# A fused MLP kernel by Strassen products: when the next x is cast, and where two weight sums stand

## The chip, the cores and the metric

The kernel runs on one core of a Trainium2 chip. The metric is device time in microseconds (us) from the first to the last instruction of one execution. The kernel before takes 1495.97 us, the median of three runs (1494.37 to 1496.18).

A core has TensorE (PE, matrix products into PSUM banks), VectorE (DVE), ScalarE (ACT) and GpSimd (POOL) as its computing engines, and SyncE (SP), which here only issues DMA transfers. Each engine works through its own instructions in order and waits on semaphores for the others. POOL issues transfers too: those that convert the type on the way (float32 to float16), and the stores of results.

## The reference

```python
h = x @ w1
h = 0.5 * h * (1 + np.tanh(np.sqrt(2 / np.pi) * (h + 0.044715 * h ** 3)))
return (h @ w2).astype(np.float32)
```

x is 8 x 1024 x 1024, w1 1024 x 4096 and w2 4096 x 1024, all float32. So it is two large matrix products with a gelu between them, over 8192 rows.

## The kernel before

The 8192 rows are taken in eight super-blocks (`sb`) of 1024. For each, `matmul1` makes g = gelu(x @ w1), kept in SBUF as float16, and then a second stage makes g @ w2. The second stage is `matmul2_made` for the first two super-blocks and `matmul2` for the others.

Every product is done in Strassen's manner: a matrix is cut into 2 x 2 blocks, called "11", "12", "21" and "22", and seven products of block sums replace eight of blocks. The products are numbered 1 to 7. The sums of weight blocks are in `W_SUM`: sum 5 is 12 - 11, sum 6 is 22 - sum 5, sum 7 is 22 - 12, sum 4 is 21 - sum 6. Those on the other side are in `S_SUM` and in `XOps.make`. Sums of weights are written w, those of x are written x, and those of g are written g below. Nearly all of these sums, and the adds that put the products together, go through the helper `tt` on line 119 to DVE. Copies from PSUM go through `act_copy` on line 135 to ACT. Loads and stores on SP go through `load_in_order` on line 132.

The order of the work on each engine is written out by hand: `tc.keep_in_program_order` pins an instruction to its place, and a table (`FILL`, and `FILL_2` for the later stages) says which extra job follows which product. A key such as `51` means: after product 5, group 1. In the first super-block and in the second, each product of the second stage has four groups (`NQ` = 4) of 16 matmuls, one group for each 128 rows.

**The start.** `First` loads the first x, transposes it on PE and loads the first weight columns. `First.pair` does the first pair of column chunks with plain products. While it runs, its function `sums` makes the x sums and the sums of the second pair of weight columns ("pair two", `(2, 2)`), in a fixed order on DVE. Then `matmul1` goes on with its loop over pairs `j` (16 chunks, 8 pairs). In one turn PE makes products 1 and 2 for both chunks of the pair, then 5, 6, 3 and 7; product 4 follows in the next turn (`late`). DVE adds products 1 and 2 together (`add(a[h], banks_b[h])`, the "chain sums"), ACT applies gelu to that and copies the other products out of PSUM. `jobs` are weight sums for later turns; the first `half` of them are put behind the chain sums and the rest at the end of the turn. For j = 1 of the first super-block `half` is 0 before.

**The second stage of the first super-block.** `matmul2_made` takes w2 in blocks: `bring` loads a block's float32 data into staging buffers (transfers `u<-in_w_dram`, 512 KB each, eight for a block) and casts each to float16. Blocks 11 and 21 are cast by POOL, block 12 by ACT, and block 22, which is brought after product 1, by ACT too. `keep` stores a cast block to `raw2_d` in DRAM (transfers `raw_d<-u`, four of 512 KB for a block), from where later stages load it. All of these are issued by SP in the order in which they are written. The seven products come in the order 1, 2, 5, 6, 3, 7, 4. Product 6 needs sum 6, so it needs block 22: jobs w60 to w63 make the four pieces of that sum after products (5, 0) and (5, 1). `post` copies a group's result out of PSUM on ACT (products 1, 5, 6 and 4) or adds it on DVE (2, 3, 7), and stores finished rows from POOL.

In the same stage the next x is made ready: `x_cast` (line 405) issues, from POOL, eight transfers that read the next 1024 rows as float32 and write them as float16 to a DRAM buffer `xb`. `after` names an instruction behind which they are placed. `x_transpose` then issues, from SP, sixteen transposing transfers from `xb` into the four x blocks. Jobs x5, x7, x6, x3 make the x sums of the next super-block; q5, q6, q7 and q4 make its first weight sums, out of a `MadeQuad` whose raw blocks are loaded from DRAM when product 3 is done (order 12, 11, 22, 21); i2 and i3 make sums of sums.

Of the kernel before, what the change touches and what calls it, by code (L numbers as in the profile page):

```python
# [29 lines left out]
def slots(table):  # L30
# [5 lines left out]
    ;20:g50 w50 w51;21:g51 w52;22:w53 g52;23:g53 p14  # L36
    ;50:w60 w61;51:w62 w63;52:g30 g31;53:g32 g33
    ;60:w70 w71;61:w72 w73;62:w40 w41;63:w42 w43
    ;70:x5;73:x7;40:x6 x3;41:q5 q6;42:q7 q4
    ;43:i2 i3""".replace("\n    ", "")),  # L40
    slots("""10:g60 w50;11:g61 w51;12:g62 w52;13:g63 w53
    ;20:g50 p55;21:g51 p56;22:g52 p57;23:g53 p54
# [19 lines left out]
def kernel(  # L62
# [7 lines left out]
    nc = tc.nc  # L70
# [38 lines left out]
    def psum():  # L109
        return pp.tile([P, HT], F32, name="ps")  # L110

    def temp():
        return tp.tile([P, HT], F32, name="tmp")

    def unit(rows, cols):
        return up.tile([P, rows, cols], DT, name="u")
# [9 lines left out]
    def flat(t):  # L126
        return t.rearrange("p a b -> p (a b)")
# [3 lines left out]
    def load_in_order(out, in_, **kw):  # L131
        return tc.keep_in_program_order(nc.sync.dma_start(out=out, in_=in_, **kw))  # L132

    def act_copy(out, in_):
        tc.keep_in_program_order(nc.scalar.copy(out=out, in_=in_))  # L135
# [8 lines left out]
    def columns(t, c, n=1):  # L144

        h, c = divmod(c, 2)
        return t[:, h * KH:(h + 1) * KH, c * P:(c + n) * P]
# [148 lines left out]
    def x_blocks():  # L296
        return {b: unit(KH, HT) for b in ("22", "21", "12", "11")}
# [8 lines left out]
    class First:  # L306
# [53 lines left out]
        def pair(self, gelu):  # L360


            def plain(bank, a, b, c, part=None):
                cols = slice(None) if part is None else slice(part * HT // 2, (part + 1) * HT // 2)
                for r in (1, 2):
                    w = columns(self.quad.raw[f"{r}{b}"], c)
                    for k in range(KH):
                        tc.keep_in_program_order(nc.tensor.matmul(  # L368
                            bank[:, cols], lhsT=w[:, k, :], rhs=self.xs.blocks[f"{a}{r}"][:, k, cols],
                            start=r == 1 and k == 0 and not part,  # L370
                            stop=r == 2 and k == KH - 1,
                            skip_group_check=bool(part),
                        ))

            def sums(h):
                for m in ("x5", "w5", "x7", "x6", "w6", "x3", "w7", "w4"):
                    if m[0] == "x":
                        self.xs.make(int(m[1]), cols=slice(h * HT // 2, (h + 1) * HT // 2), pin=True)
                    elif h == 1:
                        self.quad.sum(int(m[1]), (2, 2), True)  # L380

            for q in range(3):
                self.cast(1, q)
            for b, c in ((1, 0), (1, 1), (2, 0), (2, 1)):
                bank = psum()
                plain(bank, 1, b, c)
                if b == 2:
                    self.transpose(1, c)
                gelu(f"1{b}", c, bank)
            self.cast(1, 3)  # L390
            self.transpose(1, 2)
            banks = {(c, b): psum() for c in range(2) for b in (1, 2)}
            for part in range(2):
                for c in range(2):
                    for b in (1, 2):
                        plain(banks[c, b], 2, b, c, part)
                        if part:
                            gelu(f"2{b}", c, banks[c, b])
                    if c == 0 and not part:
                        self.transpose(1, 3)  # L400
                    if part != c:
                        self.more[part]()
                sums(part)

    def x_cast(s, after, rows=range(0, SB, P), xb=None):
        if xb is None:
            xb = xdram.tile([SB, H], DT, name="xb")
        with tc.issue_after(after.ins):
            for q in rows:
                nc.gpsimd.dma_start(out=xb[q:q + P, :], in_=x2[s * SB + q:s * SB + q + P, :])  # L410
        return xb
# [6 lines left out]
    def x_transpose(xb, dma, blocks=None, which=range(4)):  # L418
        blocks = blocks or x_blocks()
        for b, t in [list(blocks.items())[i] for i in which]:  # L420
            a, k = int(b[0]) - 1, int(b[1]) - 1
            for j in range(KH):
                dma(
                    t[:, j, :],
                    xb[a * HT:(a + 1) * HT, (k * KH + j) * P:(k * KH + j + 1) * P],
                    transpose=True,
                )
        return blocks
# [3 lines left out]
    def matmul1(xs, sb, quads, start=None):  # L432
# [69 lines left out]
        def ahead(j):  # L502

            if sb > 1 or j // 2 == NI // QC - 1:
                return ()
            q, second = divmod(j, 2)
            if not second:
                quad = MadeQuad(q + 1, sb == 0, sb == 1)
                quads.append(quad)
                if sb == 0:  # L510
                    quad.load()
                    quads[q].keep_raw()
            quad = quads[q + 1]
            if sb == 0:
                return [lambda m=m: quad.sum(m, pin=True) for m in SUMS] if second else ()
            jobs = [lambda m=m: quad.sum(m, pin=True) for m in ((7, 4) if second else (5, 6))]
            if sb == 1:
                if second:
                    jobs += [lambda m=m: quad.inner_sums(m) for m in INNER_1]
            return jobs  # L520
# [21 lines left out]
        for j in range(NI // 2):  # L542
# [11 lines left out]
            jobs = list(ahead(j))  # L554
# [5 lines left out]
            banks_c, p5, t = [], [], [temp(), temp()]  # L560
# [27 lines left out]
            difference(j - 1)  # L588
            half = (len(jobs) + 1) // 2
            if start is not None and j == 1:  # L590
                half, jobs, rest = 0, jobs[:2], jobs[2:]
            elif start is not None and j == 2:
                half, jobs = 2, rest
            if sb == 1:
                half = 3 if j % 2 else 0
# [94 lines left out]
    def matmul2_made(sb, g, keep_w1, xb):  # L690
# [24 lines left out]
        def keep(b):  # L715
            if sb == 0:
                for q in range(NI // QC):
                    load_in_order(raw2_d[q][:, BLOCKS.index(b), :], flat(raw[b][q]))
# [13 lines left out]
        def pieces(m):  # L732
            return raw[W_TERM[m]] if m in W_TERM else sums[m]

        def rows(t, q):
            return t[:, :, q * P:(q + 1) * P]

        s2, a, p5, t6, at = {}, {}, {}, {}, {}
# [47 lines left out]
        for m, name, first in (  # L786
            (1, "a", True), (2, "b", True), (5, "c", True), (6, "a", False),
            (3, "c", False), (7, "a", False), (4, "a", False),
        ):
            for q in range(NQ):  # L790
                if first:
                    banks[name].append(psum())
                bank = banks[name][q]
                matmuls2(bank, s2[q] if m == 6 else rows(g[operands[m]], q), pieces(m), first)
                post(m, q, bank)
                if (m, q) == (2, 1) and sb == 0:
                    xb = x_cast(sb + 1, at[1])
                if (m, q) == ((5, 0) if sb else (6, NQ - 1)):
                    xs = XOps(x_transpose(xb, load_in_order))
                if (m, q) == (3, NQ - 1) and sb == 0:  # L800
                    quad = MadeQuad(0, False, True)
                if (m, q) == (4, 0) and sb:
                    quad = StoredHalf(0)
                if (m, q) == (1, NQ - 1) and sb == 0:
                    sums[5] = [unit(2, HALF) for _ in range(NI // QC)]
                    for t in sums[5]:
                        act_copy(t[:, 0, :1], warm)
                    bring("22", act_copy, True)
                    for b in ("21", "12", "22"):
                        keep(b)  # L810
                run((m, q))
        return xs, [quad]

# [125 lines left out]
    def matmuls2(bank, a, pieces, first):  # L939
        for c in range(NI):  # L940
            tc.keep_in_program_order(nc.tensor.matmul(  # L941
                pair(bank),
                lhsT=a[:, c, :],
                rhs=chunks(pieces[c // QC])[:, :, c % QC, :],
                start=(first and c == 0),
                stop=(c == NI - 1),
                skip_group_check=not first,
            ))
# [75 lines left out]
    pace = consts.tile([P, 2], DT, name="pace")  # L1024
# [3 lines left out]
    xs, quads = first.xs, [first.quad]  # L1028
    for sb in range(NSB):
        g, early, nxt = matmul1(xs, sb, quads, first if sb == 0 else None)  # L1030
        if sb < 2:
            xs, quads = matmul2_made(sb, g, None if sb else quads[-1].keep_raw, nxt)
            continue
        matmul2(sb, g, early, nxt)
        if nxt is not None:
            xs, quads = nxt, [StoredHalf(0)]
# [30 lines left out]
```

## Time and profile before

| what | value |
|---|---|
| median of three runs | 1495.97 us |
| profiled execution, span | 1493.1 us |
| PE busy | 1478.2 us (99%) |
| DVE busy | 1148.6 us (77%) |
| ACT busy | 613.3 us (41%) |
| POOL busy | 226.9 us (15%) |
| HBM traffic | 313 GB/s over the span |

Where the stages lie in the span: the first multiplication of the first super-block ends and the second begins at 113.5 us; that one ends at 216.0 us; the second super-block follows, with its second multiplication from 312.9 to 409.6 us.

How to read it. Matmuls are pipelined, and their ends are modelled, so a busy PE is not a PE at its peak; but a gap in PE is time lost, as PE is busy nearly all the time. An engine's idle time costs nothing unless PE waits for it in the end. In the waits, a row names who waited, then who ended the wait, the total in us, how often, and the longest. In the timeline, "x4" means four instructions merged into one row, and the brackets give the idle time of the engine before it and what ended that. In the chain that ended last, each row is a start, a duration, and what the time was spent on. q1 is the queue of the transfers that SP issues, q0 that of those that POOL issues. The granted clock is the share of TensorE's full clock.

### The profile page before, as it was taken

The page shows a single profiled execution, that of the slowest core. Times are in us where ns is not written, and L with a number is a line of the kernel's source. Part 1 is how long each engine was busy: PE and PEld are TensorE (multiplying, and loading weights), DVE is VectorE, ACT ScalarE, POOL GpSimd, SP SyncE. Part 2 cuts the span into 40 slices and gives each one's busy share as a digit, 9 for nine tenths or more (in the row PEclk, how much of TensorE's full clock was granted, in tenths as well). Part 3 has the DMA queues.
Part 4 walks back from the last instruction along what each step waited for, and adds up shares of the span by engine and source line. Part 5 has one row for each costly group of instructions (what it writes and reads, how often), then busy time and mean ns, then how long its engine had stood idle before and what let it go on. Part 6 is the DMA issues. An engine that isn't in the chain of part 4 may idle for free.

```text
span 1493.1 us, 26323 instructions
## 1 busy us (share of the span) xinstructions
PE 1478.2 (99%) x9879; PEld 962.9 (64%) x9879; DVE 1148.6 (77%) x1792; ACT 613.3 (41%) x1154; POOL 226.9 (15%) x310
## 2 busy tenths in 40 slices
PE   8999899999999999999999999999999999999998
PEld 4444344444455788557875588755886568855687
DVE  5656448757667899778987799877997779877787
ACT  5664216531066411664126621366214652156510
POOL 2542022312311011110122001210011101101011
PEclk9999999999999999999999999999999999999999
DMA  9999996996997999999999899999999999997896
GB/s 327 335 342 365 293 333 224 390 299 233 361 309 179 340 294 308 330 219 372 310 316 322 219 381 320 294 320 247 347 303 318 290 257 361 293 375 235 295 280 216
DMA packets 242719, 453.70 MB, mean 304 GB/s; under 512 B 80672, under 2 KB 85792, under 8 KB 241696
## 3 DMA queue, kind: packets, MB, share of 16 engines
q1 hardware_dynamic: 215680, 358.69, 71.5%
q0 software_dynamic: 26912, 93.34, 21.2%
q8 instruction: 77, 1.26, 0.3%
q14 instruction: 50, 0.41, 0.1%
HBM read 355.47 MB, written 111.15 MB: 313 GB/s over the span
## 4 chain that ended last, share of the span: by engine, by line
PE 93%; DMA 4%; DVE 2%; issue 0%; ACT 0%; SPq 0%; DVEq 0%; ACTq 0%
PE ps L438 48%; PE ps L900 34%; PE ps L941 10%; DMA u<-in_w_dram 3%; DVE tmp L119 1%; PE ps L368 1%; DVE u L119 1%; DMA gc<-in_w_dram 1%; DMA u<-w_d 1%; DMA out_dram<-tmp 0%; SPq L132 0%; ACT u L135 0%; PE ps L345 0%; ACT g L451 0%; ACT tmp L135 0%
## 5 line engine op out<-in xcount | busy, mean ns | idle before, releaser
L438 PE MATMUL ps<-u 128*128 128x512 f16 (+1 forms) x4104 | 746.8, 344 | 3.4 <-DVE tmp L119 1.7
L119 DVE TENSOR_TENSOR tmp<-tmp,ps 128x256 f32<-128x256 f32 (+1 forms) x930 | 450.4, 530 | 275.7 <-PE ps L438 174.9
L438 PEld LDWEIGHTS <-u 128*128 128x128 f16 x4104 | 400.9, 98 | 346.7 <-issue 12.4
L135 ACT COPY tmp<-ps 128x512 f32<-128x512 f32 x410 | 231.1, 581 | 295.4 <-PE ps L438 154.1
L451 ACT ACTIVATE g<-tmp 128x512 f16<-128x512 f32 x378 | 238.3, 633 | 166.3 <-DVE tmp L119 166.2
L900 PE MATMUL ps<-u,gc 128*128 128x256 f16 x2688 | 300.4, 273 | 0.0
L900 PEld LDWEIGHTS <-gc 128*128 128x128 f16 x2688 | 262.5, 98 | 31.1
L119 DVE TENSOR_TENSOR u<-u 128x2048 f16<-128x2048 f16 (+3 forms) x292 | 219.6, 791 | 14.8 <-ACT u L135 12.3
L900 PE MATMUL ps<-u,g 128*128 128x256 f16 x2016 | 227.9, 273 | 0.0
L135 ACT COPY u<-ps 128x512 f32<-128x512 f32 (+1 forms) x134 | 77.9, 586 | 347.9 <-PE ps L900 341.0
L900 PEld LDWEIGHTS <-g 128*128 128x128 f16 x2016 | 197.2, 98 | 24.1
L119 DVE TENSOR_TENSOR u<-u,ps 128x512 f32<-128x512 f32 x216 | 147.3, 682 | 35.1 <-PE ps L900 28.9
L688 POOL DMA_DIRECT2D out_dram<-u x70 | 64.0, 987 | 710.8 <-DVE u L119 304.2
L941 PE MATMUL ps<-u,g 128*128 128x512 f16 x768 | 166.4, 379 | 0.0
L941 PEld LDWEIGHTS <-g 128*128 128x128 f16 x768 | 75.2, 98 | 90.6
L119 DVE TENSOR_TENSOR g<-g,g 128x2048 f16<-128x2048 f16 (+1 forms) x136 | 129.3, 972 | 1.6 <-ACT g L451 1.6
L119 DVE TENSOR_TENSOR gc<-g,gc 128x2048 f16<-128x2048 f16 x84 | 102.2, 1217 | 0.6
L119 DVE TENSOR_TENSOR gc<-g 128x2048 f16<-128x2048 f16 x78 | 94.9, 1217 | 0.0
L451 ACT ACTIVATE g<-ps 128x512 f16<-128x512 f32 x134 | 80.0, 598 | 14.6 <-PE ps L438 6.9
L138 POOL CAST u<-gc 128x1024 f16<-128x1024 f32 x40 | 47.7, 1205 | 68.2 <-DMA gc<-in_w_dram 55.6
L536 POOL TENSOR_TENSOR gc<-g 128x2048 f16<-128x2048 f16 x6 | 24.4, 4064 | 61.8 <-ACT g L451 61.8
L941 PE MATMUL ps<-u,gc 128*128 128x512 f16 x128 | 30.0, 395 | 3.8 <-DVE u L119 3.8
(36 smaller groups left out, 225.4 us busy)
## 6 DMA issues: line engine op xcount, KB each, us to landing
u<-w_d SPq DMA_DIRECT2D x336, 256.0 KB, 6.5
u<-in_d SPq DMA_DIRECT2D x168, 512.0 KB, 6.9
u<-raw_d SPq DMA_DIRECT2D x252, 256.0 KB, 7.1
out_dram<-u POOLq DMA_DIRECT2D x70, 512.0 KB, 9.4
gc<-in_w_dram SPq DMA_DIRECT2D x48, 512.0 KB, 6.2
u<-in_d SPq DMA_DIRECT2D x96, 256.0 KB, 7.2
raw_d<-u SPq DMA_DIRECT2D x32, 512.0 KB, 9.9
u<-raw_d SPq DMA_DIRECT2D x32, 512.0 KB, 12.7
```

What stands on the lines that cost most here:

```text
L119: i = nc.vector.tensor_tensor(out=out, in0=in0, in1=in1, op=op)
L135: tc.keep_in_program_order(nc.scalar.copy(out=out, in_=in_))
L138: pool_last[0] = nc.gpsimd.tensor_copy(out=out, in_=in_)
L368: tc.keep_in_program_order(nc.tensor.matmul(bank[:, cols], lhsT=w[:, k, :], rhs=self.xs.blocks[f"{a}{r}"][:, k, cols], start=r == 1 and k ...
L438: tc.keep_in_program_order(nc.tensor.matmul(bank, lhsT=w, rhs=x, start=first and k == 0, stop=k == n - 1, skip_group_check=not first,))
L451: gelu_last[0] = nc.scalar.activation(out=g[b][:, c, :], in_=src, func=GELU)
L536: nc.gpsimd.tensor_tensor(out=early[7], in0=u, in1=v, op=SUB)
L688: return nc.gpsimd.dma_start(out=rows, in_=src, **kw)
L900: tc.keep_in_program_order(nc.tensor.matmul(bank[:, i * OH // 2:(i + 1) * OH // 2], lhsT=t[:, c, i * P:(i + 1) * P], rhs=self.y[j][:, c, : ...
L941: tc.keep_in_program_order(nc.tensor.matmul(pair(bank), lhsT=a[:, c, :], rhs=chunks(pieces[c // QC])[:, :, c % QC, :], start=(first and c ...
```

## The change

Three things change, all of them in the first super-block.

1. The x cast is issued later. Before, it followed the store of group (2, 1). Now it is issued after product (5, 0) and hangs on a tiny POOL copy of `p5[0]`, the result of (5, 0) that ACT copies out of PSUM. On ACT that copy stands behind all casts of block 22. Its purpose is to let the loads of block 22 have the DMA engines to themselves. The x sums, which need the transposed x, move to later keys in `FILL` (x5 from 70 to 73, x7 from 73 to 40, x3 and q5 to 41, the other q to 42).
2. The four stores of block 22 to `raw2_d` are issued after the sixteen transposes and not before them.
3. In the first pair loop, the weight sums 7 and 4 of pair two leave the list in `sums` and are made in the turn j = 1, behind the chain sums and the difference of g and ahead of the other jobs (`half` = 2). They are wanted by product 7 of that turn and by product 4 in the next, and their purpose there is to let the chain sums go first.

The arithmetic is the same; only the order and one copy of two columns are new.

```diff
-    ;70:x5;73:x7;40:x6 x3;41:q5 q6;42:q7 q4
+    ;73:x5;40:x7 x6;41:x3 q5;42:q6 q7 q4
...
-                for m in ("x5", "w5", "x7", "x6", "w6", "x3", "w7", "w4"):
+                for m in ("x5", "w5", "x7", "x6", "w6", "x3"):
...
             if start is not None and j == 1:
-                half, jobs, rest = 0, jobs[:2], jobs[2:]
+                rest = jobs[2:]
+                half, jobs = 2, [lambda m=m: quads[0].sum(m, (2, 2), True) for m in (7, 4)] + jobs[:2]
...
-                if (m, q) == (2, 1) and sb == 0:
-                    xb = x_cast(sb + 1, at[1])
+                if (m, q) == (5, 0) and sb == 0:
+                    xb = x_cast(sb + 1, nc.gpsimd.tensor_copy(out=pace, in_=p5[0][:, :2]))
                 if (m, q) == ((5, 0) if sb else (6, NQ - 1)):
                     xs = XOps(x_transpose(xb, load_in_order))
+                    keep("22")
...
                     bring("22", act_copy, True)
-                    for b in ("21", "12", "22"):
-                        keep(b)
+                    keep("21")
+                    keep("12")
```

## The prediction

> **What bounds the kernel now.** I read the busy table and the waits of TensorE (PE) first, because they say how much there is to win at all.
>
> ```profile
> PE 1478.2 (99%) x9879; PEld 962.9 (64%) x9879; DVE 1148.6 (77%) x1792; ACT 613.3 (41%) x1154; POOL 226.9 (15%) x310
> ...
> PE ps L941 <- DVE u L119: 3.8, 2, 2.2
> PE ps L438 <- DVE tmp L119: 1.7, 6, 0.3
> PE ps L345 <- DVE tmp L337: 1.7, 4, 0.6
> PE ps L438 <- ACT tmp L135: 1.5, 1, 1.5
> ```
>
> PE is busy 1478.2 of 1493.1 us. Of the 15 us left most is the start; past it only two entries are large: 3.8 us in two waits of the second multiplication for a DVE result, and one wait of 1.5 us of the first multiplication for an ACT copy. Nothing else can be won without taking matmuls away. Next, the chain that ended last, around the 3.8 us (columns: start, duration, what).
>
> ```profile
> 140.12 1.05 ACT u L135
> 141.17 0.02 issue
> 141.19 18.13 DMA u<-in_w_dram
> 159.32 0.02 issue
> 159.34 1.05 ACT u L135
> 160.40 0.02 issue
> 160.42 1.24 DVE u L119
> 161.65 0.04 issue
> 161.70 14.37 PE ps L941 x58
> ```
>
> The last load of block 22 of w2 took 18.13 us, then its cast on ACT 1.05, then the sum w63 on DVE 1.24, and PE waited for that. The timeline tells what else ran there.
>
> ```profile
> 137.41 3.44 POOL L410 DMA_DIRECT2D xb<-in_x_dram  x7
> ...
> 151.84 1.04 ACT L135 CAST u<-u 128x1024 f16<-128x1024 f32 x1 [9.26 <-DMA u<-in_w_dram]
> ...
> 158.52 1.02 PE L941 MATMUL ps<-u,gc 128*128 128x512 f16 x4 [1.65 <-DVE u L119]
> ...
> 161.70 13.07 PE L941 MATMUL ps<-u,gc 128*128 128x512 f16 x52 [2.16 <-DVE u L119]
> ```
>
> At 137.41 POOL issues the cast of the next x. Block 22's eight casts on ACT begin at 136.82, 138.71, 140.12, 141.53 and then 151.84, 156.16, 158.07, 159.34: a hole of 10.3 us where the steps had been 1.4 to 1.9. The DMA queues from 142 to 152 us show why.
>
> ```profile
> q0 software_dynamic: 224, 1.84, 86.6%
> q1 hardware_dynamic: 224, 0.44, 12.3%
> ```
>
> The x cast (q0) holds 86.6% of the DMA time and the loads (q1) 12.3%, 0.44 MB in 10 us. From 158 to 166, with q0 empty, q1 moves 3.36 MB in 8 us: 1.25 us for a 512 KB transfer.
>
> What the stall costs in all: the windows 113.50 to 154.90 and 174.60 to 216.00 hold 12 groups of 16 matmuls each, 3.45 us a group, with no gap. The four groups of m6 between them took 19.70 us in place of 4 x 3.45 = 13.80: 5.9 us. Of this 1.65 + 2.16 = 3.8 is the two waits; the rest is a lower granted clock behind them (0.91 in that window).
>
> [...] 224 packets each, but the cast's are far larger, hence 86.6 against 12.3%. [...] here the mean clock is 0.68 from 160 to 165 us and the longest matmul 634 ns against 379. [...] two 128x1024 weight sums beside POOL's casts take 2.96 us (1.48 each), while one such operation, the difference of g, takes 0.68.
>
> **Part 1: two weight sums behind the chain sums (35 us).**
>
> ```profile
> 31.95 2.96 DVE u L119 x2
> 34.91 0.61 DVE tmp L119
> 35.52 0.02 issue
> 35.55 0.63 ACT g L451
> 36.17 0.48 ACT tmp L135
> 36.66 0.04 issue
> 36.70 1.45 PE ps L438 x6
> ```
>
> w7 and w4 (2.96 us) stand ahead of the add into a[0] (0.61). ACT, in order, waits for that add with the gelu (0.63), and behind it stands the copy of p5[1] (0.48), which PE wants before the second product 3: it waits 1.53 us. Nothing is removed or added, the two sums only move behind two adds and a difference. The chain begins 2.96 us earlier, at 31.95, so the copy ends at 36.66 - 2.96 = 33.7, before PE wants it (36.70 - 1.53 = 35.17). Saved: 1.53. The new risk is w7, which product 7 needs when product 3 is done, at 35.17 + 4 x 0.216 = 36.03. DVE: 31.95 + 1.27 (two adds) + 0.68 (difference) + 1.48 = 35.4, so 0.6 us of slack. Were w7 slowed to twice that, 0.9 us would be given back; I take 0, range 0 to 0.9. w4 is wanted only in the next pair of chunks. The sums of quad 1 after it cannot start before POOL's casts of that quad end at 41.3; no PE wait hangs on them (DVE waits for none of POOL's casts in the whole run).
>
> **Part 2: the x cast waits for p5[0].** p5[0] is ACT's copy of the first product 5. On ACT it stands behind all eight casts of block 22, so the cast begins only when block 22 is in. The queue then delivers loads 5 to 8 at 1.25 us each after 141.5. The eighth is issued at 141.19, as before (it waits for its buffer), and follows the seventh: 141.5 + 5.0 = 146.5. Other q0 work stays: two 256 KB stores and one in_d store of 512 KB, 1 MB or 2.5 us; not all of it falls ahead of the load. So it lands between 146.5 and 149, I take 147.5. Cast and w63 (1.05 + 1.24) end at 149.8. PE starts m6 at about 153.4 (154.9 - 1.5) and wants w63 twelve matmuls (2.6 us) later, at 156. Slack 6 us: both waits and the low clock go. Saved: 5.8 (19.70 less 13.80, less 0.1 for rounding of the window). The added POOL copy of two columns waits on ACT; queued behind it on POOL are only the x casts, then stores of m3 from some 170 us on. The in_d store and two stores that were behind the casts are now ahead.
>
> **Part 3: what the later cast delays.** It now starts at about 149.4 (147.5 + 1.05 + 0.6 for p5[0], 0.3 for the mark) and not at 137.41: 12 us later. Before, the last part landed 17.1 us after the first issue (137.41 to 154.5, beside q1 traffic). So it ends between 163 (10 us of pure transfer at 0.96 share, 3 us of start) and 166.5; I take 166. The transposes were issued from 165.63 before, held up there by the twelve raw_d stores of blocks 21, 12, 22 ahead of them on SP; now eight stores stand ahead, of which about three are left at 166. So the transposes start about where they did. Sixteen take 1.38 each (171.37 to 190.7 for fourteen), 22 us: the last is issued at 188 to 190, landing to 193. x5, x7, x6, x3 now come behind the last product 7, whose add ends at 203.0 - 7.3 = 195.7: nothing waits.
>
> The four stores of block 22 (2 MB, 5.0 us) now lie between the transposes and the loads of quad 0 (issued from 190.81 before). These land about 5 to 6 us later: block 11 about 204.7 for 198.8, block 21, the last, about 208.5 for 202.5. The next first multiplication starts at 216.0 - 7.3 = 208.7 with product 1 (block 11, in), product 2 (block 21) 1.7 us later at 210.4, and product 6 at 213.9 (its sum q6 ready by 208). So the slack is about 2 us. An error of that size in the cast's end is well possible; I take no wait, and keep up to 4 us for the range.
>
> **Sum.** 1.53 + 5.8 = 7.3 us. The rest of the run is PE without waits (96.7 us for 448 matmuls from 216 and again from 313), so an earlier start is passed on. 1495.97 - 7.3 = **1488.7 us**.
>
> **Rivals.** (a) Both waits go, but the quad loads come 2 to 6 us behind the new slack, so PE waits at the start of the next stage: 1488.7 + 3.5 = 1492. For it: 2 MB put ahead of loads with 2 us to spare. Against: the cast may well end at 163. (b) Block 22 stays late, since stores and the raw_d writes share the queue: half of part 2 remains, 1491.5. Against: without the cast q1 took 1.25 us per transfer, and there are 6 us of slack. (c) The other side: the cast runs some 10 us slower than before beside the raw_d writes; the transposes, the loads and the first products all slip by it: 10 - 2 = 8 us of wait plus about 2 of low clock, against 7.3 saved: 1498.7. Against: q1 got only 12.3% beside the cast, so the writes barely slow it. (d) A wait of 5 to 6 us with 2 of low clock eats the gain: 1496.
>
> **How the numbers follow.** Forecast 0.62, (a) 0.19, (b) 0.07, (c) 0.06, (d) 0.06. The low end is all of the gain plus the spread of the runs (1494.37 is 1.6 below the median): 1487.2. The high end takes in (a) and (b): 1493.0. Faster by over 3 us: forecast, (a), (b), 0.88; same 0.06; slower 0.06.
>
> **What would show it.** Right: PE's waits of 3.8 and 1.5 us gone; ACT's casts of block 22 done by about 149; the x cast issued near 149; the clock at 1.00 from 150 to 175; the next stage's first product near 208.7. Wrong: a wait of the first multiplication for a DMA of raw_d, a transpose, or a weight sum between 205 and 220 us; a wait of PE for w7 at 36; the last casts of block 22 still past 152.

## The result and the profile after

The changed kernel takes 1487.9 us (median of four runs, 1487.63 to 1488.05), beside 1495.37 us for the kernel before in the same measurement: 7.5 us or 0.5% less, ratio 0.995, 95% interval 0.9933 to 0.9967. The forecast was 1488.7.

First the busy table and the waits of PE in the changed kernel, in the same columns as those of before. (PEld is PE's loading of weights. Lines lie one or two lower in the changed kernel: L941 of before is L943 here.)

```profile
PE 1477.3 (99%) x9879; PEld 964.2 (65%) x9879; DVE 1149.5 (77%) x1792; ACT 613.3 (41%) x1154; POOL 231.8 (16%) x311
```

```profile
PE ps L438 <- DVE tmp L119: 2.3, 7, 0.6
PE ps L303 <- DVE warm L1027: 1.2, 1, 1.2
PE ps L345 <- DVE tmp L337: 0.7, 1, 0.7
PE ps L368 <- ACT u L135: 0.6, 1, 0.6
```

The two large rows are gone: 3.8 us for DVE in the second multiplication and 1.5 us for ACT at 35 us. The first row is larger than before (2.3 for 1.7): one wait at 589.8 us now takes 0.65 us for 0.29, and one of 0.16 us stood under a transfer before. PE is busy for as long as before (1477.3 against 1478.2), in a span that is 7.1 us shorter (1486.0 against 1493.1). The chain that ended last now has no transfer in the place where it had 18.13 us of one:

```profile
109.86 2.16 PE ps L438 x10
112.01 64.10 PE ps L943 x297
```

and the windows of the second multiplication show it stretch by stretch (columns: stretch, length, busy us and count of PE, PEld, DVE, ACT, POOL, then clock, DMA share, GB/s). First that of product 6 in the kernel before, then three of the changed kernel:

```profile
154.90:174.60 19.70, 15.89 (x66) 6.65 (x64) 15.41 (x14) 6.83 (x10) 0.00 (x0) 0.91 1.10 378
```

```profile
112.00:153.40 41.40, 41.40 (x194) 18.78 (x192) 31.95 (x34) 22.21 (x30) 12.58 (x14) 1.00 1.04 406
153.40:167.20 13.80, 13.80 (x66) 6.27 (x64) 8.82 (x8) 2.35 (x4) 2.26 (x5) 1.00 0.85 195
167.20:208.60 41.40, 41.40 (x194) 18.74 (x193) 15.97 (x19) 2.35 (x4) 8.11 (x15) 1.00 0.85 250
```

The four groups of product 6 take 13.80 us where they took 19.70, at a clock of 1.00 where it was 0.91. The timeline shows the two hand-overs, from the loads to the cast and from the cast to the transposes:

```profile
144.78 1.04 ACT L135 CAST u<-u 128x1024 f16<-128x1024 f32 x1 [0.22 <-DMA u<-in_w_dram]
...
146.38 5.46 POOL L798 CAST pace<-tmp 128x2 f16<-128x2 f32 x1 [2.84 <-ACT tmp L135]
...
147.16 4.62 DVE L119 TENSOR_TENSOR g<-g,gc 128x2048 f16<-128x2048 f16 x4
...
151.78 3.88 POOL L410 DMA_DIRECT2D xb<-in_x_dram  x8
...
166.59 9.68 SPq L132 DMA_TRANSPOSE u<-xb  x7
```

The last cast of block 22 begins at 144.78 and not at 159.34. The x cast has the DMA engines to itself from 156 us on. The queues from 156 to 164 us (packets, MB, share of the time of the 16 DMA engines):

```profile
q0 software_dynamic: 205, 1.69, 102.0%
q1 hardware_dynamic: 4, 0.01, 0.3%
```

### The profile page after: what moved, and what is told of

Its sections match the earlier page's. It is cut to its first block, busy times and chain, and to the rows that moved or that the text cites. A ratio compares the mean times of both kernels' runs of the same rounds, so it can differ in the third digit from the quotient of the medians.

```text
span 1486.0 us, 26324 instructions
## 1 busy us (share of the span) xinstructions
PE 1477.3 (99%) x9879; PEld 964.2 (65%) x9879; DVE 1149.5 (77%) x1792; ACT 613.3 (41%) x1154; POOL 231.8 (16%) x311
## 4 chain that ended last, share of the span: by engine, by line
PE 97%; DVE 1%; DMA 1%; issue 0%; ACT 0%; DVEq 0%
PE ps L438 49%; PE ps L902 35%; PE ps L943 13%; PE ps L368 1%; DVE tmp L119 1%; DMA out_dram<-tmp 0%; PE ps L345 0%; DMA u<-in_x_dram 0%; DVE u L119 0%; ACT u L135 0%; ACT tmp L135 0%; PE ps L303 0%; DVE tmp L337 0%; DVE u L356 0%; DVEq L119 0%
## 5 line engine op out<-in xcount | busy, mean ns | idle before, releaser
L943 PE MATMUL ps<-u,g 128*128 128x512 f16 x768 | 166.4, 379 | 0.0
L943 PEld LDWEIGHTS <-g 128*128 128x128 f16 x768 | 75.1, 98 | 90.6
L415 POOL COPY pace<-g 128x2 f16<-128x2 f16 x24 | 4.4, 185 | 191.4 <-ACT g L451 191.4
```

The source lines that it names most:

```text
L415: mark = nc.gpsimd.tensor_copy(out=pace, in_=g_chunk[:, :2])
L943: tc.keep_in_program_order(nc.tensor.matmul(pair(bank), lhsT=a[:, c, :], rhs=chunks(pieces[c // QC])[:, :, c % QC, :], start=(first and c ...
```

## The experiments

All were timed in alternation with the kernel before. There are three measurements, each with its own runs of the kernel before. These spread more widely than in the first measurement, 1490.2 to 1498.1, while the kernels without the stall stay within some 1.2 us except for single runs. So kernels without the stall are best compared with one another.

| kernel | median (range), us | before in the same measurement, us | ratio, 95% interval |
|---|---|---|---|
| weight sums moved, nothing else | 1493.43 (1490.55 to 1495.69) | 1493.65 | 0.9987 to 1.0004 |
| cast and x sums moved, nothing else | 1489.06 (1488.13 to 1489.33) | 1493.65 | 0.9951 to 0.9976 |
| stores of block 22 moved, nothing else | 1493.85 (1491.45 to 1496.65) | 1493.65 | 0.9994 to 1.0011 |
| all but the stores of block 22 | 1488.07 (1487.76 to 1489.35) | 1493.65 | 0.9948 to 0.9973 |
| changed kernel, cast still later | 1487.67 (1487.36 to 1489.66) | 1494.18 | 0.9948 to 0.9974 |
| changed kernel, mark by a transfer | 1488.43 (1487.85 to 1488.94) | 1494.18 | 0.9956 to 0.9982 |
| changed kernel, cast behind store (2, 3) | 1487.44 (1487.32 to 1487.93) | 1494.18 | 0.9946 to 0.9975 |
| changed kernel, old job keys | 1487.85 (1487.48 to 1488.06) | 1494.18 | 0.9947 to 0.9977 |
| changed kernel again | 1487.76 (1487.61 to 1488.30) | 1493.58 | 0.9947 to 0.9974 |
| changed kernel without change 3 | 1488.59 (1488.25 to 1490.21) | 1493.58 | 0.9955 to 0.9979 |
| changed kernel, cast behind store (2, 2) | 1492.99 (1489.77 to 1496.20) | 1493.58 | 0.9984 to 1.0005 |
| before, sums moved, cast behind store (2, 3) | 1487.90 (1487.47 to 1488.64) | 1493.58 | 0.9947 to 0.9976 |

**The weight sums alone.**

```diff
-                for m in ("x5", "w5", "x7", "x6", "w6", "x3", "w7", "w4"):
+                for m in ("x5", "w5", "x7", "x6", "w6", "x3"):
...
-                half, jobs, rest = 0, jobs[:2], jobs[2:]
+                rest = jobs[2:]
+                half, jobs = 2, [lambda m=m: quads[0].sum(m, (2, 2), True) for m in (7, 4)] + jobs[:2]
```

> The kernel before with change 3 alone (weight sums 7 and 4 of pair two behind the chain sums). My theory: the wait of 1.53 us at 35 goes and is kept to the end, so 1.5 us faster, with the 3.8 us of waits in the second multiplication and their low clock unchanged, since the last loads of block 22 land by the clock of the DMA queues. The rival: those loads end at a fixed time set by the DMA, so PE merely reaches the same wait 1.5 us earlier and gives the gain back there: 0 us.

Timed, 0.2 us are left of it, and the interval of the change in time (about -1.9 to +0.6 us) holds both 0 and -1.5: neither theory is settled by this. In the profile, the wait at 35 us is gone and the second multiplication begins at 111.9 and not 113.5; then PE stalls for block 22 as before, and for as long:

```profile
156.58 1.02 PE L942 MATMUL ps<-u,gc 128*128 128x512 f16 x4 [1.38 <-DVE u L119]
160.06 13.07 PE L942 MATMUL ps<-u,gc 128*128 128x512 f16 x52 [2.46 <-DVE u L119]
```

In that one profile the lead was kept (span 1491.7 against 1493.1). The rival's step, that loads end at a fixed time, is not what it shows: the cast is issued behind PE's result (2, 1), so it too came 1.4 us earlier (136.0 against 137.4), and the last load landed 1.6 us earlier (157.7 against 159.3). But the stall itself differs from run to run by more than 1.5 us, so the part can only be measured where the stall is gone; see below.

**The cast alone, and everything but the stores.** The first has only the two edits shown here; the second has those and the weight sums.

```diff
-    ;70:x5;73:x7;40:x6 x3;41:q5 q6;42:q7 q4
+    ;73:x5;40:x7 x6;41:x3 q5;42:q6 q7 q4
...
-                if (m, q) == (2, 1) and sb == 0:
-                    xb = x_cast(sb + 1, at[1])
+                if (m, q) == (5, 0) and sb == 0:
+                    xb = x_cast(sb + 1, nc.gpsimd.tensor_copy(out=pace, in_=p5[0][:, :2]))
```

> The kernel before with the x cast and the sums of x moved as in the change, the stores of block 22 still ahead of the transposes, the two weight sums as before. My theory: the cast is the whole cause of the late block 22, so both waits (3.8 us) and the low clock go: 5.8 us faster, and the wait of 1.5 us at 35 stays. The rival, that the stores of block 22 have to go behind the transposes for this: transposes and first products of the next super-block come late, under 4 us gained.

> The changed kernel with the stores of block 22 put back ahead of the transposes. My theory: when the cast ends at 166 the twelve stores have hardly anything left, so the transposes start at most 3 us later, within slack, and the time is that of the changed kernel, 7.4 us below before (within 0.5). The rival: the four stores now meet the cast in the queue and the transposes start some 5 us later, past the slack: 1 to 4 us slower than the changed kernel.

The cast alone gives 4.6 us (1493.65 - 1489.06) by the medians, with an interval of 3.6 to 7.3; 5.8 is the stall of the one profile of before. The waits for block 22 are gone, and the wait at 35 us stands at 0.7 us. With the weight sums too, 1488.07: as fast as the changed kernel, whose two measurements gave 1487.9 and 1487.76. The rival of this second run, and with it the step on which that of the first rests, is refuted: the stores of block 22 may stay ahead of the transposes.

**The stores of block 22 alone.**

```diff
-                    for b in ("21", "12", "22"):
-                        keep(b)
+                    keep("21")
+                    keep("12")
...
                     xs = XOps(x_transpose(xb, load_in_order))
+                    keep("22")
```

> The kernel before with the stores of block 22 behind the transposes, and nothing else. My theory: block 22 is late because of the cast, so nothing changes in the waits: within 0.5 us of before. The rival, that the order of the stores is part of the gain: 1 us or more faster.

Nothing in time (1493.85 beside 1493.65). Its profile is of use all the same: here PE waited once, for 2.10 us, at the same place, and the chain had a load of 18.24 us.

```profile
155.00:171.50 16.50, 14.40 (x68) 6.45 (x66) 12.82 (x12) 5.92 (x10) 0.00 (x0) 1.00 1.00 327
```

The clock stayed at 1.00. From the first matmul of this multiplication to the first of the next it took 99.0 us, where the changed kernel takes 96.7: 2.3 us lost, hardly more than the wait. Before, two waits of 1.65 and 2.16 cost 5.8. So the stall of the same loads cost 2.3 us here, in one wait and with the clock at 1.00, and 5.8 before, in two waits and with the clock at 0.91. The spread of the kernel before fits this. Of its 55 timed executions in the three measurements, 18 have a mean granted clock of 1.000 and take 1490.2 to 1492.9 us, 19 have 0.999 and take 1491.8 to 1495.1, and 18 have 0.998 and take 1493.9 to 1498.1. These are means over a whole execution, so they do not show where the clock was lost.

**How late may the cast be?** The mark is taken from t6[0], the result of (6, 0).

```diff
-                if (m, q) == (5, 0) and sb == 0:
-                    xb = x_cast(sb + 1, nc.gpsimd.tensor_copy(out=pace, in_=p5[0][:, :2]))
+                if (m, q) == (6, 0) and sb == 0:
+                    xb = x_cast(sb + 1, nc.gpsimd.tensor_copy(out=pace, in_=t6[0][:, :2]))
```

> The changed kernel with the cast hung on the result of product (6, 0), about 11 us after that of (5, 0), so that the cast starts some 6 us or more later (at 157.6 or after). It measures the slack behind the cast. In the changed kernel block 21 of quad 0 lands at 206.4 and product 2 of the next stage wants it at 210.3, so the slack is 3.9 us. My theory: the shift passes on one to one through transposes, stores and loads, so PE waits for the shift less 3.9: 2 us lost if the cast starts at 157.6, up to 8 plus some low clock if the mark is held up longer. The rival, that the queue has room between and absorbs it: no loss.

The cast starts at 158.47, 6.7 us later, and its last part lands at 173.5 for 166.4; the last transpose is 6.5 us later (193.4 for 186.9). The last block of quad 0, though, lands at 210.6 for 206.4, only 4.2 us later: the queue between them had room. What PE feels of it is one wait:

```profile
210.69 4.49 PE L438 MATMUL ps<-u 128*128 128x512 f16 x20 [0.27 <-DMA u<-raw_d]
```

0.27 us, lost in the noise of the time (1487.67). My theory, a shift passed on one to one, would have lost 2.8 us at this start (6.7 less 3.9) and was wrong: of the shift 2.5 us were absorbed and 3.9 were slack.

**Another mark.** `mark_d` is a small new buffer in DRAM.

```diff
-                    xb = x_cast(sb + 1, nc.gpsimd.tensor_copy(out=pace, in_=p5[0][:, :2]))
+                    xb = x_cast(sb + 1, nc.gpsimd.dma_start(out=mark_d, in_=p5[0][:, :2]))
```

> The changed kernel with another mark: a transfer from POOL that reads the same two columns of p5[0], in place of the POOL copy. In the changed kernel that copy of two columns stands in the profile with 5.46 us, from 146.4 to 151.8, just until DVE ends four operations on two SBUF inputs. My theory: the copy was held up by DVE, so a mark without a POOL read starts the cast at about 147 and it lands some 4 us earlier, as do transposes and loads; the time stays within 0.5 us, as they had slack. The rival, that the copy's span is only badly recorded or that POOL waits for something else: the cast starts at 151 to 152 again.

The first cast is issued at 147.66, right after the mark, so POOL was free at that time and the copy was indeed what held it. But the last one goes out at 158.80 and lands at 169.7, later than with the copy (166.4):

```profile
147.66 2.94 POOL L411 DMA_DIRECT2D xb<-in_x_dram  x6
153.13 0.49 POOL L411 DMA_DIRECT2D xb<-in_x_dram  x1 [2.53 <-DMA in_d<-u]
158.80 0.49 POOL L411 DMA_DIRECT2D xb<-in_x_dram  x1 [5.18 <-DMA mark_d<-tmp]
```

The last two parts wait for transfers issued from POOL eight before them, the last of all for the mark itself. Half of the expectation failed: an earlier start was no earlier end. The time, 1488.43, is 0.5 and 0.7 us above the two medians of the changed kernel, which were taken in other measurements. With ranges that overlap, this cannot be told from 0.

**How early may the cast be?** In the changed kernel, the cast is put right behind a store of product 2, with no mark; first behind that of group (2, 3), then (2, 2).

```diff
-                if (m, q) == (5, 0) and sb == 0:
-                    xb = x_cast(sb + 1, nc.gpsimd.tensor_copy(out=pace, in_=p5[0][:, :2]))
+                if (m, q) == (2, 3) and sb == 0:
+                    xb = x_cast(sb + 1, at[3])
```

> The changed kernel with the cast placed right behind the store of group (2, 3), without any mark, at about 143 to 144. My theory: what matters is only that the last load of block 22 is on its way before the cast's data flows (3 us after issue); that load lands at 144.8 in the changed kernel, so there is no wait to speak of and the time is that of the changed kernel within 0.5 us. The rival, that the cast has to wait for all casts of block 22: the last loads are slowed and 1 to 3 us are lost.

> The changed kernel with the cast right behind the store of group (2, 2), one group (3.5 us) earlier than behind (2, 3), where PE did not wait and the last load landed at 149.6. My theory: the last load is slowed by the cast's first data and lands at 152 to 155; w63 is wanted at 156 and takes 2.3 us after the landing, so PE waits 0 to 2 us: 0 to 2 us slower than the changed kernel, and no clock loss, as the wait is short. The rival, that any overlap of cast and loads brings the whole stall back: 4 us or more slower.

Behind (2, 3) the cast is issued from 142.06 and the last load lands at 149.6, when its cast on ACT begins:

```profile
149.60 1.04 ACT L135 CAST u<-u 128x1024 f16<-128x1024 f32 x1 [3.27 <-DMA u<-in_w_dram]
```

That is 4.8 us later than in the changed kernel, so this load was slowed, against the expectation; but PE needs it only at about 153.4 and does not wait. (An estimate: product 6 begins at 153.1 and wants the last piece of its sum twelve matmuls, 2.6 us, later; the load's cast and that piece take 2.3 us.) The time, 1487.44, is the lowest median of all, though only 0.3 below the changed kernel in another measurement. One group earlier, from 139.81, nearly all of the stall is back, 1492.99. There the queues from 145 to 155 us, PE's wait and the window of product 6 read:

```profile
q0 software_dynamic: 260, 1.83, 83.2%
q1 hardware_dynamic: 262, 0.54, 14.9%
```

```profile
PE ps L943 <- DVE u L119: 4.1, 1, 4.1
```

```profile
153.40:172.60 19.20, 15.11 (x64) 6.45 (x63) 12.84 (x12) 5.80 (x9) 0.00 (x0) 0.91 1.01 316
```

Loads 7 and 8 of block 22, still out in this window, came in at 155.7 and 158.7, when the cast was done or nearly so (its last part landed at 156.0). I had expected 152 to 155 and a wait of at most 2 us, and was wrong: it is a cliff between issues at 139.8 and at 142.1. The packet records of the traces show the reason. The first packet of the cast's data comes 1.2 to 4.9 us after its first issue in the fourteen profiles (3.6 in the kernel before, 1.9 in the changed one); here it came at 142.3, when loads 5 to 8 had not landed, and behind (2, 3) at 146.4, when only load 8 had not.

**The job keys of before.** Only the `FILL` line is put back in the changed kernel.

```diff
-    ;73:x5;40:x7 x6;41:x3 q5;42:q6 q7 q4
+    ;70:x5;73:x7;40:x6 x3;41:q5 q6;42:q7 q4
```

> The changed kernel with the sums of x and the q sums at the keys of before (x5 after product (7, 0), x7 after (7, 3)). My theory: all transposes land by 190.1, blocks 22 and 21 by 179.7, before those keys come up, so nothing changes: within 0.5 us of the changed kernel. The rival, that DVE then stands waiting for a transpose and holds up the adds of product 7: 0.5 to 3 us slower.

1487.85: no difference. The moved keys are a precaution that these transposes do not need.

**What is the weight sums' part worth?** The changed kernel, and the changed kernel with the lists of change 3 put back.

> The changed kernel itself, beside the next three on the same chip. Both theories: 1487.9 within 0.5 us; before lies between 1490 and 1496, as its stall differs from run to run.

> The changed kernel without change 3: the weight sums 7 and 4 of pair two stand again ahead of the chain sums. It settles what change 3 is worth once the later stall is gone. My theory: the wait at 35 comes back, 0.7 us (as where the cast alone was moved) to 1.5 us (as before), and is kept to the end: 0.7 to 1.5 us slower than the changed kernel. The rival, that it is made up later: no difference.

1487.76 against 1488.59: 0.8 us, with ranges that hardly meet. (The kernel before reached 1498.1 beside them, above the 1496 that I had expected of it.) PE's wait at 36 us is back:

```profile
27.82 6.83 DVE L119 TENSOR_TENSOR u<-u 128x1024 f16<-128x1024 f16 x7 [1.00 <-ACT u L196]
...
36.43 0.81 PE L438 MATMUL ps<-u 128*128 128x512 f16 x3 [0.69 <-ACT tmp L135]
```

The wait is 0.69 us here, and was 1.53 in the profile of before. The seven sums ahead of the chain sums took 6.83 us here and 7.66 there: the difference of 0.83 is just that of the waits (0.84). While they ran, POOL made four casts there, and three and the beginning of a fourth here. No run takes the casts away, so whether they lengthen the sums is not shown. In two profiles each the wait was 0.69 (this one and the cast alone) and 1.53 to 1.55 (before and the stores alone).

**The shortest version.** The kernel before with change 3 and one edit more:

```diff
-                if (m, q) == (2, 1) and sb == 0:
-                    xb = x_cast(sb + 1, at[1])
+                if (m, q) == (2, 3) and sb == 0:
+                    xb = x_cast(sb + 1, at[3])
```

> The kernel before with change 3 and with the cast behind the store of group (2, 3) in place of (2, 1), all else as before: no mark, the stores of block 22 ahead of the transposes, the sums of x at their old keys. My theory: those other parts do nothing for the time, so it is as fast as the changed kernel within 0.5 us. The rival, that stores of block 22 ahead of the transposes meet the cast and hold up DVE at the old keys: 1 us or more slower.

1487.90, as fast as the changed kernel. Moving the cast by two groups does all that the mark, the moved stores and the moved keys do. In its profile the cast is issued from 141.1 and the last load lands at 145.3, so the cliff lies between issues at 139.8 and at 141.1. As it is one group away, the mark of the changed kernel, which follows the loads wherever they fall, should be the safer form; no run here tests that.

## Why the prediction was right

The mechanism of the forecast held: both waits and the low clock went, and nothing came late behind the moved cast. That its sum, 7.3 us, was met so closely, by 7.5 in the first measurement, is in part luck. By the later ones, in which the kernel before had medians of 1493.6 to 1494.2, the gain is nearer to 6 (1493.58 - 1487.76 = 5.8). Both terms were read from one execution, which took 1494.86 us, and were taken off the median of others, 1495.97, whose stalls were not known; taken off 1494.86 they give 1487.6. The changed kernel took 1487.9 and 1487.76.

- **Part 1, 1.53 us: the mechanism held, the term was too large.** The copy that PE had waited for is no longer late; measured where nothing else stalls, the part is worth 0.8 us. The wait in the profile of before was one case of a wait that is 0.7 or 1.5 us. The risk that was named, product 7 waiting for w7, is real and small: 0.20 us in the kernel without the moved stores, none in the matmuls of the changed kernel. One reading was not clean: the difference of g, set at 0.68 us against 1.48 for a sum beside POOL's casts, itself ran beside such a cast, which began 0.24 us after it (36.27 against 36.03). In the kernel without change 3 the same operation took 1.49.
- **Part 2, 5.8 us: right, with the waits and the clock together.** The groups of product 6 went from 19.70 to 13.80. That is the stall of that profile; over many runs the cast alone gave 4.6. The last load landed at 144.8, earlier than the 147.5 worked out. It was issued at 138.14, not at 141.19: I had held its issue fixed, but the casts that free its buffer came earlier too. In the second profile of the changed kernel it was issued at 139.8 and landed at 147.1.
- **Part 3, the later cast: it costs nothing, as said; in the first profile two errors cancelled.** The cast started at 151.8 for the 149.4 said, because POOL's copy of two columns took 5.46 us; the 0.3 set for it was an estimate that no trace had shown. It ended at 166.4 for the 166 said, as it took 14.7 us and not 16.6, with q1 at 0.3% from 156 to 164. In the second profile the copy took 0.75 us, the cast started at 149.4 and ended at 166.5, as worked out. The quad's last block landed at 206.4 for 208.5, so the slack was 3.9 us and not 2. The later cast showed that even 6.7 us more cost PE only 0.27.
- **The rivals.** (a) and (c) needed slack that runs out; the late cast shows how far off that was. (b), that block 22 stays late beside the other traffic, did not come about, nor did the long wait of (d). The moved stores were given no cost and the moved keys no wait, and the runs that take them back agree.

Part 2 was carried by what the queues of the kernel before showed: as many packets from each, but 86.6 and 12.3% of the time. The early cast shows it once more: 260 packets of one queue and 262 of the other in 10 us, with 83.2 and 14.9% of the time. What sets the order of the packets is not shown; the shares go with their sizes. The packet records of the kernel before, from 142 to 152 us, give the sizes: half of the cast's 224 packets are of 16 KB and took 1.23 us each, the other half are of 4 bytes; nearly all of the loads' 224 are of 2 KB and took 0.09 us each.

## What to carry to other kernels

When a load that PE will wait for shares the DMA engines with a large transfer on another queue, look at the packets and the time of each queue in that window: with 224 packets each in 10 us, the queue with the larger ones took 86.6% of the time here and the other 12.3%. Issue the large transfer so that its data begin to flow when the last urgent load is about to land, and find the cliff by moving it a step to both sides; here one group (issues at 139.8 and 142.1) was worth nearly all of the stall, while an issue 16 us later still, at 158.5, cost nothing that the times show. A gain that lies ahead of a stall of varying length is measured only once that stall is gone.

## What the runs showed of the hardware

- The second multiplication of the first super-block took 96.7 us from its first matmul to the first of the next stage where PE did not wait. A wait of 2.10 us left the clock at 1.00 and made it 99.0, so it cost 2.3 us in all. With two waits of 1.65 and 2.16, or 1.38 and 2.46, and about 1 us of matmuls between, and with one wait of 4.09, the mean clock over product 6 was 0.91 and the multiplication took 102.5: each time 5.8 us more, so 1.7 to 2 us beyond the waits. In the kernel before, the granted clock was 0.50 from 161.8 to 165.3 us, from just after the second wait on, and 1.00 in the rest of product 6; in the slow part a matmul took up to 634 ns for 379. What idle time it takes to bring the clock down is not shown beyond these cases.
- POOL's copy of 128 x 2 elements took 5.46 and 5.66 us in two profiles, 0.75 us in four and 0.95 us in one. In all seven it ended 0.04 to 0.05 us after the end of a DVE operation on SBUF. In the five short cases the copy came up during an operation that DVE had begun after a pause (0.02 us in the case of 0.95, 0.8 to 1.4 us in the others), and it ended with that operation. In the two long ones DVE was in an unbroken run of operations, and the copy ended when the run did. Why the copy ends with DVE's work, and what decides whether with one operation or with the whole run, is not settled here.
